# A small extra read of fifteen partitions behind the first load of a row softmax

## The chip, the core and the metric

The kernel runs on one core of a Trainium2 chip. The metric is the device time of one execution in microseconds (us), as a median over runs. The core has several engines with their own instruction streams: VectorE (DVE), ScalarE (ACT), GpSimd (POOL) and SyncE (SP). Data moves between the chip's memory and the core's on-chip buffers by 16 DMA engines; SyncE and ScalarE issue the transfers here, each on a queue of its own.

## The reference

```
B, H, S = 2, 8, 2112
bias   = rel_bias[:, clip(pos[:, None] - pos[None, :], -16, 16) + 16]     # H x S x S
logits = logits + bias[None]                                              # B x H x S x S, float32
out    = softmax(logits, axis=-1)
```

There are 2 x 8 x 2112 = 33,792 rows of 2112 numbers. Each row gets a bias that depends only on the head and on the clipped distance between the row's position and the column, and then a softmax over the row. All data is float32: 285 MB are read and 285 MB written.

## The kernel before

The 33,792 rows are divided among 128 partitions, 264 rows (`ROWS`) in sequence on each. A step takes R = 6 rows of every partition: one load of 128 x 12,672 numbers into one of four buffers `X[0]` to `X[3]` (`NBUF` = 4), so that there are 44 steps, 11 passes over the four buffers. In each partition the load is one contiguous piece of 50,688 B.

The work of a step, with its lines:

- SyncE issues the load (`load`, L78). In the first pass it issues four loads back to back (L106); after that it waits for the buffer's previous store (`take(nc.sync, st[b], 16)`) and issues the next load into it. `take`, L74, is every wait on a semaphore that is counted down again.
- VectorE waits for the load (`ld[b]`), then adds the bias to each of the six rows and takes its maximum in the same instruction (`add`, L175). The bias comes from a strip `F` that is copied once per pass from a table in PSUM (L169).
- ScalarE takes the exponential of each row, with the row's sum (`exps`, L184).
- VectorE takes reciprocals and scales the rows in two halves (`scale`, L192 and L196).
- ScalarE waits for the six scaled rows and issues the store (`store`, L82). The last step's store is issued in two halves of three rows.

Everything happens in the order in which it is written on each engine. Loads lie on SyncE's DMA queue (q1 in the profile) and stores on ScalarE's (q10); both run on the same 16 DMA engines. A DMA raises its semaphore by 16 in all, and a buffer counts as loaded or stored at the full 16. Ahead of the loops, VectorE builds the bias table from `rel_bias`, which ScalarE loads (L100).

Of the kernel before, what the change touches and what calls it, by code (L numbers as in the profile page):

```python
# [15 lines left out]
def kernel(  # L16
# [6 lines left out]
    nc = tc.nc  # L23
    P = 128
    B, H, S, S2 = logits.shape
# [3 lines left out]
    ROWS = B * H * S // P  # L29
    PB = S // ROWS  # L30
    assert ROWS * P == B * H * S and PB * ROWS == S and PB == H == 8
    R = 6
    NBUF = 4
# [4 lines left out]
    MW = S + ROWS - 1  # L38
    FW = S + STEP - 1
    BIG = 3.0e38  # L40

    io = ctx.enter_context(tc.tile_pool(name="io", bufs=1))
    X = [io.tile([P, R * S], FP32, tag=f"X{b}", name=f"X{b}") for b in range(NBUF)]
# [9 lines left out]
    def view(t, offset, dims):  # L53

        return bass.AP(tensor=t.tensor, offset=t.offset + offset, ap=[[list(t.ap[0])[0], P]] + dims)

    def rows(t, j, n):

        return bass.AP(tensor=t.tensor, offset=t.offset + j * S, ap=[[ROWS * S, P], [1, n * S]])

    with tc.tile_critical(no_gpsimd_drain=True):  # L61
# [6 lines left out]
        rb = nc.alloc_semaphore("rb")  # L68
        idx = nc.alloc_semaphore("idx")
        dve = nc.alloc_semaphore("dve")  # L70
        landed = tc.alloc_semaphore("landed")

        def take(eng, sem, n):
            eng.wait_ge(sem, n).then_inc(sem, -n)  # L74


        def load(j, b):
            nc.sync.dma_start(out=X[b][:, :], in_=rows(logits, j, R)).then_inc(ld[b], 16)  # L78
# [15 lines left out]
        def settle():  # L94
# [6 lines left out]
            out=bass.AP(tensor=F.tensor, offset=F.offset, ap=[[PB * list(F.ap[0])[0], P // PB], [1, H * W]]),  # L101
            in_=bass.AP(
                tensor=rel_bias.tensor, offset=rel_bias.offset, ap=[[0, P // PB], [1, H * W]]
            ),
        ).then_inc(rb, 16)
        for n in range(NBUF):  # L106
            load(n * R, n)

        nc.gpsimd.iota(ip[:, 0], pattern=[[0, PB]], base=0, channel_multiplier=1).then_inc(idx, 1)
        nc.gpsimd.iota(ip[:, 2], pattern=[[1, PB]], base=0, channel_multiplier=0).then_inc(idx, 1)  # L110
# [16 lines left out]
        for m, op in ((eq, ALU.is_equal), (gt, ALU.is_gt), (le, ALU.is_le), (lt, ALU.is_lt)):  # L127
# [4 lines left out]
            out=view(F, 0, [[W, H], [1, W]]), in0=view(F, 0, [[W, H], [1, W]]),  # L132
# [8 lines left out]
                           in_=view(F, RT, [[Q, 2], [PB, Q // PB], [0, PB]])))  # L141
# [9 lines left out]
            out=view(F, 0, [[W, PB], [1, W]]), in0=view(F, SC + 2 * PB, [[1, PB], [0, W]]),  # L151
# [7 lines left out]
            out=view(M, U, [[ROWS, PB], [1, W]]), in0=view(F, 0, [[W, PB], [1, W]]),  # L159
            in1=view(F, SC + 8 * PB, [[1, PB], [0, W]]), op=ALU.add))  # L160
        then(v.tensor_copy(out=view(M, U + W, [[ROWS, PB], [1, ROWS - W]]),  # L161
                           in_=view(F, SC + 7 * PB, [[1, PB], [0, ROWS - W]])))
# [8 lines left out]
        def add(b):  # L171
            take(v, ld[b], 16)
            for r in range(b * R, (b + 1) * R):
                x = X[b][:, (r - b * R) * S : (r - b * R + 1) * S]
                v.tensor_tensor_reduce(  # L175
                    out=x, in0=x, in1=F[:, STEP - 1 - r : STEP - 1 - r + S], scale=-1.0, scalar=BIG,
                    op0=ALU.add, op1=ALU.min, accum_out=nmax[:, r : r + 1],
# [76 lines left out]
```

## Time and profile before

| | |
|---|---|
| median of 3 runs | 1332.47 us (1328.36 to 1335.96) |
| the profiled execution | 1331.85 us, of which the span of the trace is 1330.0 us |
| VectorE busy | 977.7 us (74%) |
| ScalarE busy | 574.3 us (43%) |
| moved by DMA | 570.99 MB, mean 429 GB/s over the span |
| a load, issue to landing | 37.4 us (median) |
| a store, issue to landing | 60.2 us (median) |

The span runs from the first to the last instruction; the execution's own time is 1.85 us longer. In a row of the sums by window, the columns are the window, its length, busy time and instruction count of DVE, ACT and POOL, the clock granted to TensorE (unused here), and the busy share and rate of the DMA engines. In the page's groups the time behind the last bar is how long the engine sat idle ahead of these instructions, and what ended it. A row of the timeline gives start, duration, engine, line and operation; a "q" behind an engine's name is its sequencer, which issues DMAs.

### The profile page before, as it was taken

To read this page: it belongs to the slowest core of one execution; us is meant where nothing else is said; L and a number is where in the kernel's file an instruction comes from. 1 tells how busy PE (TensorE), PEld (TensorE's weight loads), DVE (VectorE), ACT (ScalarE), POOL (GpSimd) and SP (SyncE) were. 2 spreads that over 40 slices of the span, in tenths; PEclk is the share of its full clock that TensorE was granted. 3 is DMA by queue.
4 is the path that set the end of the run, shared out by engine and by line. 5 is a ranking of instruction groups with operands and counts; after the bars stand their busy time and mean duration, and the time that the engine had idled before them with its cause. 6 is when DMAs were issued, how large, how long until landed. Compare 5 with 4: busy or idle time off the path is not lost. (4 is left out here: it accounts for less than half of the span.)

```text
span 1330.0 us, 2473 instructions
## 1 busy us (share of the span) xinstructions
DVE 977.7 (74%) x917; ACT 574.3 (43%) x538; POOL 0.4 (0%) x6
## 2 busy tenths in 40 slices
DVE  7998767677877776687778767677877777677773
ACT  3474333444444343344444333444444443333442
POOL 0000000000000000000000000000000000000000
DMA  9999999999999999999999999999999999999997
GB/s 414 416 436 427 430 438 439 433 425 434 439 436 431 428 436 436 439 431 424 439 438 434 430 430 436 439 433 430 430 438 434 427 428 438 436 438 428 428 438 308
DMA packets 12850, 570.99 MB, mean 429 GB/s; under 512 B 1440, under 2 KB 1456, under 8 KB 1456
## 3 DMA queue, kind: packets, MB, share of 16 engines
q1 hardware_dynamic: 6336, 285.48, 49.8%
q10 hardware_dynamic: 6512, 285.49, 49.6%
q14 instruction: 2, 0.02, 0.0%
HBM read 285.49 MB, written 285.47 MB: 429 GB/s over the span
## 5 line engine op out<-in xcount | busy, mean ns | idle before, releaser
L175 DVE CUSTOM_DVE_ANT_0 X<-X,F 128x2112 f32<-128x2112 f32 x264 | 605.2, 2354 | 310.1 <-DVEq L74 310.1
L184 ACT ACTIVATE X<-X,nmax 128x2112 f32<-128x2112 f32 x264 | 541.7, 2052 | 559.0 <-ACTq L74 539.0
L196 DVE TENSOR_SCALAR X<-X,rec 128x2112 f32<-128x2112 f32 x264 | 332.5, 1316 | 13.2
L184 ACT ACT_TABLE_LOAD x10 | 12.8, 1283 | 170.8 <-ACTq L74 170.8
L184 ACT ACTIVATION_READ_ACCUMULATOR X<-X,nmax 128x1 f32 x264 | 49.2, 186 | 0.0
L169 DVE COPY F<-M 128x2135 f32 x11 | 26.1, 2374 | 0.5 <-DVEq L198 0.5
L175 DVE DVE_READ_ACCUMULATOR2_ANT nmax<- 128x1 f32 x264 | 21.6, 82 | 0.0
L192 DVE RECIPROCAL rec<-tot 128x3 f32<-128x3 f32 x88 | 14.9, 170 | 0.0
L131 DVE TENSOR_TENSOR F<-F 128x264 f32<-128x264 f32 x1 | 0.4, 433 | 7.0 <-DMA F<-in_rel_bias_dram 7.0
L161 DVE COPY M<-F 128x1848 f32<-128x1848 f32 x1 | 2.1, 2077 | 0.0
L97 DVE MEMSET F<- 128x264 f32 x1 | 0.3, 278 | 1.1 <-SPq L61 1.1
L135 DVE TENSOR_REDUCE F<-F 128x33 f32<-128x264 f32 x1 | 0.6, 608 | 0.0
L158 DVE TENSOR_TENSOR M<-F 128x264 f32<-128x264 f32 x1 | 0.4, 441 | 0.0
L150 DVE TENSOR_TENSOR F<-F,rbS 128x264 f32<-128x264 f32 x1 | 0.4, 426 | 0.0
L128 DVE TENSOR_SCALAR F<-F 128x8 f32<-128x8 f32 x4 | 0.4, 165 | 0.0
L163 DVE COPY M<-rbS 128x247 f32<-128x247 f32 x1 | 0.4, 407 | 0.0
L143 DVE STREAM_TRANSPOSE F<-F 128x64 f32<-128x64 f32 x1 | 0.2, 246 | 0.0
L138 DVE STREAM_TRANSPOSE F<-F 128x64 f32<-128x64 f32 x1 | 0.2, 245 | 0.0
L148 DVE TENSOR_SCALAR F<-F,rbS 128x8 f32<-128x8 f32 x1 | 0.2, 231 | 0.0
L154 DVE SCALAR_TENSOR_TENSOR F<-F,rbS 128x8 f32<-128x8 f32 x1 | 0.2, 227 | 0.0
L149 DVE TENSOR_SCALAR F<-F,rbS 128x8 f32<-128x8 f32 x1 | 0.2, 225 | 0.0
L155 DVE SCALAR_TENSOR_TENSOR F<-F,rbS 128x8 f32<-128x8 f32 x1 | 0.2, 221 | 0.0
(15 smaller groups left out, 2.1 us busy)
## 6 DMA issues: line engine op xcount, KB each, us to landing
X<-in_logits_dram SPq DMA_DIRECT2D x44, 6336.0 KB, 37.4
out_dram<-X ACTq DMA_DIRECT2D x43, 6336.0 KB, 60.2
out_dram<-X ACTq DMA_DIRECT2D x2, 3168.0 KB, 17.3
F<-in_rel_bias_dram ACTq DMA_DIRECT2D x1, 16.5 KB, 8.0
```

The lines of the kernel that those rows point to most:

```text
L128: then(v.tensor_scalar(out=m, in0=dp, scalar1=0.0, scalar2=None, op0=op))
L131: then(v.tensor_tensor(out=view(F, 0, [[W, H], [1, W]]), in0=view(F, 0, [[W, H], [1, W]]), in1=view(F, SC + 3 * PB, [[1, H], [0, W]]), op= ...
L135: then(v.tensor_reduce(out=F[:, RB : RB + W], in_=view(F, 0, [[1, W], [W, H]]), axis=mybir.AxisListType.X, op=ALU.add))
L150: then(v.tensor_tensor(out=view(F, 0, [[W, PB], [1, W]]), in0=view(F, SC + 2 * PB, [[1, PB], [0, W]]), in1=view(rbS, W - 1, [[0, PB], [-1, ...
L158: then(v.tensor_tensor(out=view(M, U, [[ROWS, PB], [1, W]]), in0=view(F, 0, [[W, PB], [1, W]]), in1=view(F, SC + 8 * PB, [[1, PB], [0, W]] ...
L161: then(v.tensor_copy(out=view(M, U + W, [[ROWS, PB], [1, ROWS - W]]), in_=view(F, SC + 7 * PB, [[1, PB], [0, ROWS - W]])))
L163: then(v.tensor_copy(out=M[:, 0:U], in_=low.to_broadcast([P, U])))
L169: v.tensor_copy(out=F[:, :], in_=M[:, bass.ds(ROWS - STEP - j, FW)]).then_inc(dve, 1)
L175: v.tensor_tensor_reduce(out=x, in0=x, in1=F[:, STEP - 1 - r : STEP - 1 - r + S], scale=-1.0, scalar=BIG, op0=ALU.add, op1=ALU.min, accum_ ...
L184: nc.scalar.activation(out=x, in_=x, func=EXP, scale=-1.0, bias=nmax[:, r : r + 1], accum_out=tot[:, r : r + 1],).then_inc(expd, 1)
L192: v.reciprocal(out=rec[:, r0 : r0 + HALF], in_=tot[:, r0 : r0 + HALF]).then_inc(inv, 1)
L196: v.tensor_scalar_mul(out=x, in0=x, scalar1=rec[:, r : r + 1]).then_inc(scaled, 1)
```

## The change

Behind load 0, SyncE issues one more DMA. It reads 2,560 numbers (10,240 B) for each of fifteen partitions, 32, 36, and so on to 88, into `X[3]`: the first part of what load 3 brings to these partitions. Load 3 comes after loads 1 and 2 as before, but now behind a wait for a new semaphore `even`, which the extra DMA raises. Load 3 overwrites the same places with the same data, so that the extra DMA adds nothing to the result.

```diff
+    LOW, PAD = 32, 2560
 ...
+        even = nc.alloc_semaphore("even")
 ...
-        for n in range(NBUF):
+        load(0, 0)
+        pad = X[NBUF - 1]
+        nc.sync.dma_start(
+            out=bass.AP(tensor=pad.tensor, offset=pad.offset + LOW * list(pad.ap[0])[0],
+                        ap=[[4 * list(pad.ap[0])[0], 15], [1, PAD]]),
+            in_=bass.AP(tensor=logits.tensor, offset=logits.offset + (LOW * ROWS + (NBUF - 1) * R) * S,
+                        ap=[[4 * ROWS * S, 15], [1, PAD]]),
+        ).then_inc(even, 16)
+        for n in range(1, NBUF - 1):
             load(n * R, n)
+        take(nc.sync, even, 16)
+        load((NBUF - 1) * R, NBUF - 1)
```

On SyncE, ahead of its loop, the instructions of before stand like this (`X_58` to `X_61` are the four buffers `X[0]` to `X[3]`; the branch behind them enters the loop):

```order
L249 UNCONDITIONAL_BRANCH
L78 DMA X_58<-in_logits_dram 128x12672
L78 DMA X_59<-in_logits_dram 128x12672
L78 DMA X_60<-in_logits_dram 128x12672
L78 DMA X_61<-in_logits_dram 128x12672
L97 UNCONDITIONAL_BRANCH
```

And after the change, with the line numbers of the changed kernel:

```order
L261 UNCONDITIONAL_BRANCH [waits SP_sequencer_49]
L80 DMA X_58<-in_logits_dram 128x12672
L110 DMA X_61<-in_logits_dram 15x2560
L80 DMA X_59<-in_logits_dram 128x12672
L80 DMA X_60<-in_logits_dram 128x12672
L80 DMA X_61<-in_logits_dram 128x12672 [waits even]
L99 UNCONDITIONAL_BRANCH
```

Loads 1 to 3 stand one place further back, and the load into `X_61` waits; the other engines' instructions, and SyncE's loop, are as before.

## The prediction

> **What bounds the kernel now.** I read the page first: the line of GB/s over the span, the DMA queues, and the groups of lines with what ended their idle time.
>
> ```profile
> span 1330.0 us, 2473 instructions
> ...
> DMA  9999999999999999999999999999999999999997
> ...
> q1 hardware_dynamic: 6336, 285.48, 49.8%
> q10 hardware_dynamic: 6512, 285.49, 49.6%
> ...
> L175 DVE CUSTOM_DVE_ANT_0 X<-X,F 128x2112 f32<-128x2112 f32 x264 | 605.2, 2354 | 310.1 <-DVEq L74 310.1
> ...
> X<-in_logits_dram SPq DMA_DIRECT2D x44, 6336.0 KB, 37.4
> out_dram<-X ACTq DMA_DIRECT2D x43, 6336.0 KB, 60.2
> ```
>
> The 16 DMA engines are busy from end to end, half of their time for loads (q1) and half for stores (q10). VectorE waits 310.1 us in front of its add (L175), released each time through L74, the wait for a load. So the transfers are the bound. The second view, the sums by window, gives their pace, and shows start and end.
>
> ```profile
> 0.00:42.00 42.00, 32.20 (x48) 13.63 (x13) 0.42 (x6) 1.00 0.96 406
> 300.00:500.00 200.00, 149.29 (x138) 88.57 (x84) 0.00 (x0) 1.00 1.00 434
> ...
> 1.95:2.30 0.35, 0.32 (x6) 0.00 (x0) 0.00 (x0) 1.00 7.14 2172
> 2.30:3.00 0.70, 0.16 (x3) 0.00 (x0) 0.00 (x0) 1.00 0.00 0
> 3.00:3.10 0.10, 0.00 (x0) 0.00 (x0) 0.00 (x0) 1.00 1.41 507
> ...
> 1322.20:1324.20 2.00, 0.00 (x0) 0.00 (x0) 0.00 (x0) 1.00 0.12 51
> 1324.40:1328.80 4.40, 0.00 (x0) 0.00 (x0) 0.00 (x0) 1.00 0.05 23
> 1328.80:1330.00 1.20, 0.00 (x0) 0.00 (x0) 0.00 (x0) 1.00 0.00 0
> ```
>
> The last two columns are the DMA engines' busy share and the GB/s, counted at the packets' starts. In the middle the engines move 434 GB/s at a share of 1.00. At the start, a packet is one partition's 6336.0 KB / 128 = 50,688 B. From 1.95 to 2.30 us, 2172 GB/s x 0.35 us = 760 KB: fifteen packets. Then nothing starts until 3.00, and 507 GB/s x 0.10 us is one packet. So one engine begins about 1 us after fifteen others. At the end a share of 0.12 is two engines of 16, and about 0.06 is one: fourteen engines are done by 1322.2 us, a fifteenth by 1324.4, and the sixteenth works alone until 1328.8. The bytes are the same for each engine, so the last one is about 6.6 us behind the fourteen, and the end waits for it.
>
> Where does it fall behind? A load counts as landed when its last engine is done, so the late engine sets when VectorE starts, and so when ScalarE issues the store. The timeline of ScalarE has these issues, one per buffer.
>
> ```profile
> 135.70 0.34 ACTq L82 DMA_DIRECT2D out_dram<-X  x1
> ...
> 316.30 0.34 ACTq L82 DMA_DIRECT2D out_dram<-X  x1
> ...
> 675.60 0.34 ACTq L82 DMA_DIRECT2D out_dram<-X  x1
> ...
> 1190.40 0.34 ACTq L82 DMA_DIRECT2D out_dram<-X  x1
> ...
> 1280.08 0.34 ACTq L82 DMA_DIRECT2D out_dram<-X  x1
> ```
>
> One load and one store at 434 GB/s take 2 x 6,488,064 B / 434 GB/s = 29.90 us; call it a step. From 135.70 to 316.30 are 6 steps: 180.60 us, 1.2 more than 6 x 29.90. The next 12 take 359.30, 0.5 more. The 17 to 1190.40 take 514.80, 6.5 more. The last 3 take 89.68, nothing more. In total 8.2 us over 38 steps. The pace of all engines together stays at 434, yet the pace of the latest one slips, and in bouts: that is the only sizeable loss after the start.
>
> **The change part by part.** *The extra DMA itself.* Fifteen rows of 10,240 B, behind load 0 and ahead of load 1 on SP's queue. One engine's share of 434 GB/s is 27.1 GB/s, so a row takes 0.38 us on its engine; none of the rows here is of that size. The nearest above is the first packet of an engine, from the start's window: 7.14 x 0.35 x 16 / 15 = 2.67 us for five times the bytes, 0.54 us at that rate. Below, no engine that carries a row can gain by it. I take 0.38, since the queue is already running when the rows come (bounds 0.38 to 0.54). Fifteen engines thereby do everything later by that, and one does not: the 1 us by which the late one started becomes 0.6.
>
> Which engines take the rows is not seen in this trace. By the Trainium skill (DMA: Bandwidth & Descriptors, "Why a DMA increments its semaphore by 16 and not by 1"), a DMA of SyncE runs on the largest number up to 16 that divides its slowest dimension, on the lowest-numbered engines: fifteen here, one each. No run here shows it yet. That the sixteenth is the one that starts late is my inference.
>
> *SP's queue.* One more issue ahead of loads 1 to 3, then the wait for `even` ahead of load 3.
>
> ```profile
> L78 SPq DMA_DIRECT2D X<-in_logits_dram x44: 332/333/737, 1.0 to 1250.7; - x44
> ...
> SPq L74 <- SPq L74: 131.6, 3, 72.8
> ...
> 40.65 2.35 DVE L175 CUSTOM_DVE_ANT_0 X<-X,F 128x2112 f32<-128x2112 f32 x1
> ...
> 84.06 2.35 DVE L175 CUSTOM_DVE_ANT_0 X<-X,F 128x2112 f32<-128x2112 f32 x1
> ...
> 113.67 2.36 DVE L175 CUSTOM_DVE_ANT_0 X<-X,F 128x2112 f32<-128x2112 f32 x1 [5.54 <-DVEq L74]
> ```
>
> An issue takes 0.33 us, and loads 1 and 2 are only queued behind load 0 then. The wait ends when the rows have landed: load 0 occupies about 2 us plus 6.49 MB / 434 GB/s = 15 us, so at about 19 us, issue included. Queued behind the wait on SP are load 3 and the loop's first wait for a store; that wait lasts 72.8 us anyway (the longest of SP's), so SP is free. Loads 1 and 2 are another 30 us of transfers, so the engines still have work until about 48 us when load 3 joins at 19. VectorE starts on load 1 at 40.65 and on load 3 at 84.06 without a wait; its first wait for data after load 0 is at 113.67. Cost of issue and wait: 0. If load 3 joined only after load 2 had drained, the cost would be the gap, up to a load's latency.
>
> *The lag.* The lag grew by 1.2 us in the first bout, little for 12 steps, then 6.5. My reading: being behind is what makes an engine slower, since its packets then meet the others' turn from one buffer or direction to the next. An engine that starts 0.6 us back instead of 1 sits inside the field, and the chain to the long bout does not start. Then no engine ends later than the fourteen did, give or take a packet. The sum on the profiled execution: last packet at 1322.2 + 0.38 for the rows + 1.2 from there to the span's end = 1323.8, against 1330.0: -6.2 us. Also the fourteen idled shortly before the end, because the last store came late:
>
> ```profile
> 1305.00:1307.50 2.50, 2.35 (x4) 0.00 (x0) 0.00 (x0) 1.00 0.57 243
> ```
>
> 0.43 of 2.5 us is 1.1 us of mean idle time, which goes too when the last load no longer lands late. Together -7.3 us. The steps say the same from the other side: 8.2 - 0.38 = 7.8 if all the slip goes, 7.0 if the 1.2 of the first bout stays. The profiled execution took 1331.85 us, 1.85 more than its span; it becomes 1324.55. It lies 0.6 below the median of 1332.47, so the forecast is 1325.2 us, -0.55%.
>
> **The rivals.** *The lag has another cause, and nothing changes (0.20).* The late engine may be slow by itself, or be slowed by which addresses it reads at that time, whatever its phase. Then it does the same packets with the same losses, its own queue is not longer, and the end stays: 1332.5 us. For it: the slip comes in bouts, as addresses go by. Against a steady handicap: twelve steps in a row cost only 0.5 us more than the engines' mean pace, which an always slower engine could not do.
> The Trainium skill (DMA: Bandwidth & Descriptors, "Latency and other measured facts") has engines 7 and 15 as usually slower than the rest, with a best guess at the cause that concerns the software queue alone. By that rule 15 stays last; the page shows only hardware queues and instruction fetches here, so its guessed cause is absent, and the twelve steps speak against it.
>
> *The rows miss their mark (0.07).* If the late engine is among the fifteen, or the fifteen rows all lie on one or a few engines, the late one is delayed too: 1332.5 + 0.4 = 1332.9 us, up to 15 x 0.38 = 5.7 more if one engine carries all, and the load behind waits for it: 1338.2.
>
> *Another phase is worse: slower (0.18).* What decides may be the phase between one engine and the fifteen, not its sign. The place is the long bout. Its mean price is 6.5 / 17 = 0.38 us a step, and in its steepest part
>
> ```profile
> 886.44 0.34 ACTq L82 DMA_DIRECT2D out_dram<-X  x1
> ...
> 1129.94 0.34 ACTq L82 DMA_DIRECT2D out_dram<-X  x1
> ```
>
> 8 steps take 243.50 us, 4.3 over 239.2, so 0.54 each. If the new phase meets this price from the start, 38 steps cost 14.4 to 20.5 us instead of 8.2: 1338.7 to 1344.8 us, about 1341. It decides for "slower" from (8.2 + 6.7) / 38 = 0.39 us a step. For it: the three runs of before already lie between 1328.36 and 1335.96, so the slip varies by some 4 us each way without a change.
>
> **How the numbers follow.** The forecast's case has 0.55. Its own range goes from 1324.3 (all 8.2 us gone) to 1328.1, where the late engine is cured but the fifteenth, done at 1324.4, stays: 1324.4 against 1328.8 is -4.4. Half a per cent, about what a measurement of this kernel can tell from no change, is 6.7 us, so the threshold is 1325.8, inside this case: 0.45 of its 0.55 fall below, 0.10 within. With the 0.20 and the 0.07 that is 0.37 for the same. Slower has 0.18. The range reaches from 1322.0 (1324.3, with half of the lower spread of before's runs) to 1341.0, the middle of the slower case.
>
> **What would show it.** In the profile after, right would be: one engine's packets alone in the last microseconds gone, so that the DMA share falls from near 1 to 0 within about 3 us of the end; store issues 29.9 to 30.0 us apart all the way; a DMA of 15 rows that lands near 19 us; no wait of VectorE ahead of its second to fourth buffer. Wrong would be: the same long tail at a share of 0.06 with the last packet near 1329, or steps of 30.3 us and more again, or from early on.

## The result, and the profile after

| | before | after |
|---|---|---|
| median | 1334.87 us (9 runs, 1328.36 to 1336.56) | 1327.46 us (9 runs, 1326.46 to 1328.63) |
| the profiled execution | 1331.85 us, span 1330.0 | 1327.58 us, span 1325.7 |

The ratio is 0.9946, with a 95% interval from 0.9932 to 0.9961: faster by 0.54%. The spreads matter as much as the medians. Three more sets of runs of the kernel before, made beside the experiments, hold 31, 35 and 35 runs from 1326.37 to 1338.20 us, and 17, 16 and 16 of them lie over 1332 us; the others lie mostly between 1326 and 1330. I call these the upper and the lower group. The change has no run over 1328.63. It does not make the best executions faster; it removes the upper group. The profiled execution of before lies between the two groups, so the two traces differ by 4.3 us of span where the medians differ by 7.4.

The sums by window of the changed kernel show the end:

```profile
1305.00:1307.50 2.50, 2.48 (x3) 0.00 (x0) 0.00 (x0) 1.00 1.06 456
1320.70:1322.40 1.70, 0.00 (x0) 0.00 (x0) 0.00 (x0) 1.00 0.17 75
1322.80:1324.40 1.60, 0.00 (x0) 0.00 (x0) 0.00 (x0) 1.00 0.07 32
1324.50:1325.70 1.20, 0.00 (x0) 0.00 (x0) 0.00 (x0) 1.00 0.00 0
```

No engine idles at 1305 us any more (share 1.06, counted at the packets' starts, where before had 0.57). At 1320.7 us some three engines of 16 are left (0.17), and one alone works from 1322.8 (0.07) until about 1324.4: a tail of nearly 4 us, where before the last engine had trailed by 6.6. The store issues in ScalarE's timeline show where the tail stopped growing:

```profile
137.96 0.34 ACTq L84 DMA_DIRECT2D out_dram<-X  x1
...
320.21 0.34 ACTq L84 DMA_DIRECT2D out_dram<-X  x1
...
679.73 0.34 ACTq L84 DMA_DIRECT2D out_dram<-X  x1
...
1188.10 0.34 ACTq L84 DMA_DIRECT2D out_dram<-X  x1
...
1277.67 0.34 ACTq L84 DMA_DIRECT2D out_dram<-X  x1
```

The first 6 steps take 182.25 us, 2.9 more than 6 x 29.90. The next 12 take 359.52, much as before. The 17 to 1188.10 take 508.37, just 17 x 29.90; before they took 514.80. The long bout is gone. The DMA issues on the two pages hold the clue to why. Before:

```profile
X<-in_logits_dram SPq DMA_DIRECT2D x44, 6336.0 KB, 37.4
out_dram<-X ACTq DMA_DIRECT2D x43, 6336.0 KB, 60.2
```

and after:

```profile
X<-in_logits_dram SPq DMA_DIRECT2D x44, 6336.0 KB, 40.9
out_dram<-X ACTq DMA_DIRECT2D x43, 6336.0 KB, 56.4
...
X<-in_logits_dram SPq DMA_DIRECT2D x1, 150.0 KB, 17.5
```

The last column is the median time from issue to landing. Loads land 3.5 us later and stores 3.8 us earlier, in the median over the run. An engine that alternates between the queues moves one packet of each in 2 x 1.87 us (50,688 B at 27.1 GB/s), so this is about an offset of one packet: the two streams stand differently against each other on at least one engine. One engine is enough for that, because a load has landed only when its last engine is done. Where it happened is seen in the DMA packets that start between 46.4 and 48.3 us, soon after the first store was issued. Before:

```profile
DMA packets 16, 0.81 MB, mean 427 GB/s; under 512 B 0, under 2 KB 0, under 8 KB 0
...
q10 hardware_dynamic: 16, 0.81, 98.5%
```

and after:

```profile
q10 hardware_dynamic: 15, 0.76, 92.4%
q1 hardware_dynamic: 1, 0.05, 9.0%
```

Before, all 16 engines start a store packet (q10) there. After, one engine is reading (q1) while the others store: between 44.95 and 46.4 us one store packet had already started, where before no packet starts at all:

```profile
q1 hardware_dynamic: 1, 0.05, 11.8%
q10 hardware_dynamic: 1, 0.05, 8.1%
```

The engines then alternate: from 48.3 to 50.2 us, 15 of them start a load packet and one a store packet, so the one keeps its offset. A load raises its semaphore in 16 steps, whose times are in the trace. For load 2, which lands next, 15 of them come by 53.80 us and the last at 55.94; before, all 16 had come by 53.62. I call this a split meeting.

### The profile page after: what moved, and what is told of

Read it like the earlier page. It is cut to its first block, busy times and chain, and to the rows that moved or that the text cites. A ratio compares the mean times of both kernels' runs of the same rounds, so it can differ in the third digit from the quotient of the medians.

```text
span 1325.7 us, 2475 instructions
## 1 busy us (share of the span) xinstructions
DVE 977.9 (74%) x917; ACT 574.3 (43%) x538; POOL 0.4 (0%) x6
## 6 DMA issues: line engine op xcount, KB each, us to landing
X<-in_logits_dram SPq DMA_DIRECT2D x44, 6336.0 KB, 40.9
out_dram<-X ACTq DMA_DIRECT2D x43, 6336.0 KB, 56.4
X<-in_logits_dram SPq DMA_DIRECT2D x1, 150.0 KB, 17.5
```

## The experiments

Three sets of runs on three chips follow; each ratio compares a variant with the runs of the kernel before in its own set. In the variants with extra rows the change's DMA is written as a function, `again(partition, step, rows, column, length)`; where only a number differs, the diff shows it as it would stand in the change.

Theories at first: *lateness* (the prediction's: the late sixteenth engine is given its start back), *issue or wait*, *any extra bytes*. After the first four, one more: the *meeting* theory, by which only the offset between the load and the store stream counts. All variants keep the kernel's own work. "Delay" edits are made in the kernel before unless said otherwise. The two numbers behind each are the median landing times of loads and stores on its page.

**The rows made tiny.**

```diff
-    LOW, PAD = 32, 2560
+    LOW, PAD = 32, 128
```

> The fifteen rows are 512 B instead of 10,240 B, so that the issue, the semaphore and load 3's wait stay and the shift of fifteen engines falls from 0.38 us to about 0.02. Lateness theory (the engine that starts last must be given back its start): no gain, ratio to before 0.998 to 1.002, about 1334 us. Issue theory (the later load 3 or the extra issue does it, not the bytes): the gain stays, ratio 0.993 to 0.996, about 1327 us.

Measured: 1332.11 us, ratio 0.9989 (0.9964 to 1.0013), 6 of 12 runs over 1332; landings 37.5 and 60.3. Issue, semaphore and wait alone give no clear gain.

**Sixteen rows: every engine shifted alike.**

```diff
-                        ap=[[4 * list(pad.ap[0])[0], 15], [1, PAD]]),
+                        ap=[[4 * list(pad.ap[0])[0], 16], [1, PAD]]),
 ...
-                        ap=[[4 * ROWS * S, 15], [1, PAD]]),
+                        ap=[[4 * ROWS * S, 16], [1, PAD]]),
```

> Sixteen rows of 10,240 B instead of fifteen, so that every engine is shifted by the same 0.38 us. Lateness theory: the last engine stays as far behind the others as before, ratio 0.998 to 1.003, about 1334 to 1335 us, with a tail of one engine of some 5 us or more. Theory that any short transfer at this place helps by breaking the rhythm: ratio 0.993 to 0.996, about 1327 us.

Measured: 1327.06 us, ratio 0.9958 (0.9938 to 0.9977), 1 of 12 over 1332; landings 39.8 and 57.4. The gain is there with no engine given anything back: the lateness theory has failed. Between 44.95 and 46.4 us its packets are

```profile
q10 hardware_dynamic: 10, 0.51, 80.7%
q1 hardware_dynamic: 5, 0.25, 48.7%
```

ten store packets and five reads: ten of the 16 engines take the store a packet earlier than the others.

**Twice the rows' length.**

```diff
-    LOW, PAD = 32, 2560
+    LOW, PAD = 32, 5120
```

> Fifteen rows of 20,480 B, a shift of 0.76 us instead of 0.38. Lateness theory: the engine without a row is then about level with the first of the others, nobody is later than before by more than 0.4 us, so the time is that of the change within 0.4 us: about 1327 to 1328 us, ratio 0.993 to 0.996. Theory that one particular phase between the one and the fifteen decides: another phase gives another time, back toward 1334 us (ratio over 0.998) or lower than the change (ratio under 0.993).

Measured: 1329.42 us, ratio 0.9971 (0.9953 to 0.9988), 1 of 12 over 1332; landings 41.0 and 56.4. About half the gain. In the same window all 16 engines start the store, one packet earlier than before: the streams are offset, without a split.

**The change, and two engines made late.**

```diff
+        again(LOW, 4, 2, 2560, 5120)
 ...
-        take(nc.sync, even, 16)
+        take(nc.sync, even, 32)
```

> The change, and behind its fifteen rows two rows of 20,480 B more, on two engines, which are thereby 0.76 us later than the rest. Lateness theory: the lag comes back on one of these two, the time returns to that of before, ratio 0.997 to 1.003, about 1332 to 1336 us. Theory that the sixteenth engine alone is special: two other engines may be late without harm, the gain stays, ratio 0.993 to 0.996, about 1327 us.

Measured: 1327.28 us, ratio 0.9948 (0.9929 to 0.9967), 0 of 8 over 1332; landings 39.9 and 57.2. Two engines 0.76 us later than the rest do no harm: the second blow to lateness.

**Rows as long as a packet.**

```diff
-    LOW, PAD = 32, 2560
+    LOW, PAD = 32, 12672
```

> Fifteen rows of 50,688 B, the size of one packet of a load, so that fifteen engines are shifted by one whole packet (1.87 us) and their packet boundaries stand against the first store as in the kernel before. Theory of the meeting (what counts is where in its run of read packets an engine is when the first store reaches it, since engines then alternate between reading and writing): all or nearly all engines meet the store alike, as before, no gain from it, and the rows cost 1.9 us: ratio 0.999 to 1.004, about 1335 us. Theory that extra bytes at this place help as such: ratio 0.993 to 0.998, about 1328 us.

Measured: 1329.16 us, ratio 0.9986 (0.9966 to 1.0006), 1 of 12 over 1332. The first store is met alike (16 store packets from 46.4 to 48.3 us), but the landings are 40.1 and 57.3: the load queue is one packet longer on these engines, which offsets the streams from then on. I had not thought of that; I read the time as the lower group's plus most of the rows' own 1.9 us.

**VectorE held up, no extra reads.**

```diff
         settle()
+        then(v.memset(F[:, 0:470], 0.0))        # then 1065, then 1660
+        settle()
 
         def strip(j):
```

> The kernel before without any extra read; VectorE fills 470 numbers of the strip's buffer ahead of its loop (about 0.45 us), so that the first store is issued that much later while the loads run as before. Meeting theory: the boundaries stand 0.45 us earlier against the store, the other way from the change's 0.38, so no certain gain: ratio 0.995 to 1.003. Theory that extra bytes or a shift of the loads are needed: ratio 0.998 to 1.002, about 1334 us.

> The same with 1,065 numbers, about 0.95 us. Meeting theory: the first store meets the engines half a packet later in their reads than in the kernel before, and at one of the three delays (0.45, 0.95, 1.45 us) the engines must split, some taking the store one packet earlier than others; there the ratio is 0.992 to 0.997, about 1326 to 1329 us. Theory that extra bytes are needed: ratio 0.998 to 1.002, about 1334 us, at all three.

> The same with 1,660 numbers, about 1.45 us, which is a packet of 1.87 us less the change's shift of 0.38 to 0.42: the boundaries stand against the store as in the change. Meeting theory: the gain of the change without its bytes, ratio 0.992 to 0.996, about 1326 to 1329 us. Theory that extra bytes are needed: ratio 0.998 to 1.002, about 1334 us.

The first store is issued at 40.99 us before and at 41.12, 41.76 and 42.34 in these three. The shortest delay thus barely moved it. Measured: 1334.54 us (ratio 1.0004, 0.9976 to 1.0032), 1330.46 (1.0007, 0.9983 to 1.0031) and 1327.34 (0.9982, 0.9962 to 1.0003); over 1332 are 7, 5 and 1 of 12, against 16 of 35 of the kernel before beside them. The first two have landings of 37.3 and 60.2, 37.2 and 60.1. The third has

```profile
X<-in_logits_dram SPq DMA_DIRECT2D x44, 6336.0 KB, 34.4
out_dram<-X ACTq DMA_DIRECT2D x43, 6336.0 KB, 63.1
```

offset the other way, and from 46.4 to 48.3 us

```profile
q10 hardware_dynamic: 13, 0.66, 80.1%
q1 hardware_dynamic: 3, 0.15, 24.0%
```

three engines reading once more. A fill on VectorE that moves the first store by 1.35 us thus comes to the change's median without an added byte. Its ratio's interval just reaches 1, so the count over 1332 says more here than the ratio.

**The change, with the store put back.** The same fill, of 800 numbers, in the changed kernel; its first store is issued at 41.66 us instead of 41.11.

> The change, and VectorE fills 800 numbers ahead of its loop, so that the first store comes about 0.5 us later and meets the engines' packet boundaries as in the kernel before, all of them alike; the sixteenth engine still has its 0.38 us back. Meeting theory (a split meeting gives the gain): the two groups of runs of the kernel before are back, near 1327 and near 1335 us, median 1329 to 1335, at least 3 of 12 runs over 1332. Lateness theory (the sixteenth engine's start gives it): the change's times, all runs within 1326 to 1330 us.

Measured: 1333.32 us, ratio 1.0012 (0.9986 to 1.0039), 6 of 12 over 1332, in two groups (1326.63 to 1330.99 and 1335.65 to 1336.77). The rows are read as in the change, with the same 150 KB, and the gain is gone. The page has

```profile
X<-in_logits_dram SPq DMA_DIRECT2D x44, 6336.0 KB, 37.3
out_dram<-X ACTq DMA_DIRECT2D x43, 6336.0 KB, 60.2
...
X<-in_logits_dram SPq DMA_DIRECT2D x1, 150.0 KB, 17.5
```

the landings of the kernel before, and from 46.4 to 48.3 us all 16 engines start a store packet again:

```profile
q10 hardware_dynamic: 16, 0.81, 98.5%
```

This profile is of a run of the lower group (1328.64 us), and so is that of the 0.95 us delay (1327.76). Landings as in step are thus seen in short executions too; they do not tell which group an execution falls in. Of all the runs this one tells the theories apart best, with a reservation: the change was not run again in this set, and its 0 of 9 is from another one.

**Sixteen rows as long as a packet.** The rows' count 16 and length 12,672.

> Sixteen rows of 50,688 B: every engine one packet later, none ahead, and the first store met as in the kernel before. Against the fifteen rows of this size only the sixteenth engine differs. Lateness theory: two groups of runs, 1.9 us above those of the kernel before, near 1329 and 1337 us, median 1331 to 1337, some runs over 1335. Meeting theory with equal meeting also gives two groups, then the fifteen rows' lack of runs over 1334 stays unexplained by it; a result like the fifteen rows (all under 1334) would speak for the bytes or the wait instead.

Measured: 1330.30 us, ratio 0.9987 (0.9969 to 1.0006), all between 1328.23 and 1333.70; landings 44.7 and 52.6. As with the fifteen, no run is over 1334, so once more nothing is seen to hang on the sixteenth engine. Four of 12 are over 1332; less the rows' 1.9 us, none is over 1331.8. I expected two groups; with the streams offset by two packets (7.3 us in the landings) it has one wide one. It was not the equal meeting that I meant to make either: besides the longer load queue, one engine took the store a packet early, as in the change (15 store packets from 46.4 to 48.3 us). And its profiled execution (1332.85 us) has a DMA share of only 0.28 from 1305.0 to 1307.5 us, so offset streams are not free of the loss.

**A longer delay.** Two fills of 1,210 numbers; the first store is issued at 43.32 us.

> The kernel before with VectorE held up by about 2.3 us ahead of its loop (two fills of 1,210 numbers), a whole packet and some more, so that the first store finds all engines one read packet further on, but again all alike. Meeting theory: two groups of runs as in the kernel before, at least 3 of 12 over 1332 us, median 1328 to 1336. Theory that a later first store helps as such (the delay of 1.45 us did): all runs 1326 to 1330 us.

Measured: 1328.96 us, ratio 0.9984 (0.9961 to 1.0006), 4 of 12 over 1332 in a spread from 1326.95 to 1335.92; landings 37.3 and 60.8, close to before. So a late store is no clear gain as such; four of twelve against one of twelve is a weak difference by itself, but it goes with the landings. Its profiled execution (1335.92 us) shows the tail, in the sums by window:

```profile
1305.00:1307.50 2.50, 2.35 (x5) 2.37 (x3) 0.00 (x0) 1.00 0.14 61
...
1328.00:1332.80 4.80, 0.00 (x0) 0.00 (x0) 0.00 (x0) 1.00 0.06 26
```

Most engines wait at 1305 us for the last store (share 0.14), and one works alone up to 1332.8.

**Two engines late, no fifteen rows.** The change's DMA with 2 rows of 5,120 numbers.

> No fifteen rows; only two rows of 20,480 B, so that two engines are 0.76 us later and the other fourteen meet the store as in the kernel before. Lateness theory: engines that are late from the start become the stragglers every time, the lower group vanishes: median 1333 to 1338 us, ratio 1.000 to 1.006. Meeting theory: as before, or better if the two split off: ratio 0.994 to 1.001.

Measured: 1329.82 us, ratio 1.0002 (0.9978 to 1.0026), 4 of 12 over 1332 (all four over 1336); landings 38.7 and 58.3. The lower group has not vanished, against lateness. The two late engines did split off in the profiled execution (2 store packets between 44.95 and 46.4 us), and yet the upper group is there: with two of sixteen the meeting is not enough, or does not come about in every run.

## Why the prediction was right, and where its reason was not

*The time.* 1325.2 us was forecast and 1327.46 measured, in the range; -0.55% and -0.54%. The agreement is partly luck: the sum on the profiled execution gave -7.3 us, and that pair of traces has -4.3. It misses 3.0 us because it let all engines end with the fourteen, while one still trails until 1324.4. The medians differ by 7.4 because the runs of before lie higher than its profiled one: the median of the nine is 1334.87, that of the three from which the forecast set out 1332.47. Of the signs that the prediction named, the rows' landing near 19 us came; the others did not all come. One engine still works alone at the end, the first six steps are 30.4 us apart, and VectorE waits ahead of its fourth buffer.

Two of its sums are slightly off by their own terms, without weight for the result: 7.0 for the steps with the first bout kept leaves out the 0.38 (6.6), and the lower bound of the range would be 1322.2, not 1322.0.

*What bounds the kernel, and where it loses.* Right. In the two traces the gain is the bout from 675 to 1190 us (6.5 us before, nothing after) and, with it, the idle time at 1305 us. The small growth in the first steps did not go: 1.2 us before, 2.9 after.

*The costs of the extra read.* Right in that they cost nothing in the end, but not in the detail. VectorE still starts its second buffer without a wait; for the fourth, which the prediction saw ready too, it waits 1.75 us:

```profile
40.77 2.35 DVE L187 CUSTOM_DVE_ANT_0 X<-X,F 128x2112 f32<-128x2112 f32 x1
...
86.01 2.36 DVE L187 CUSTOM_DVE_ANT_0 X<-X,F 128x2112 f32<-128x2112 f32 x1 [1.75 <-DVEq L76]
```

SyncE's wait for `even` is not the reason: with the tiny rows, which keep it, VectorE starts this buffer at 83.98 us without a wait. Of load 3's 16 semaphore steps, 15 come by 83.95 us and the last at 85.83, later than any of before's (83.58); that it is the engine of the split meeting is likely, but not shown. The DMA engines stay busy meanwhile (433 GB/s at a share of 1.00 from 60 to 120 us).

The rows landed 17.5 us after an issue at 1.4 us, at 18.9, as worked out. One size was off: this DMA's issue on SyncE took

```profile
L110 SPq DMA_DIRECT2D X<-in_logits_dram x1: 982/982/982, 1.4 to 1.4; - x1
```

0.98 us instead of 0.33; SyncE had nothing else to do. The packets that start from 17.4 to 18.8 us in the changed kernel are

```profile
DMA packets 62, 0.96 MB, mean 689 GB/s; under 512 B 31, under 2 KB 31, under 8 KB 31
```

31 of them small. A load has 16 small packets beside its 128 rows (6,336 packets for 44 loads are 144 each), so 16 belong to load 0 and 15 to the rows. So the rows ran on fifteen engines, as the Trainium skill (DMA: Bandwidth & Descriptors, "Why a DMA increments its semaphore by 16 and not by 1") has it. Which fifteen, no run shows.

*The step that failed* is the one under "The lag": that an engine 0.6 us back instead of 1 sits inside the field and so escapes. Sixteen rows, which leave every engine as far back as it was, had the gain. The change with its store delayed by 0.55 us kept the fifteen rows and lost it. And a delay of VectorE by 1.45 us had no run but one over 1332 with no rows at all. The traces show it directly in the times at which the 16 semaphore steps of a store come. In the store that lands at 676 us, the last step is 2.2 us behind the median of the 16 before the change and 2.1 us after it, so the last engine had not moved into the field. In the one that lands at about 1280 us it is 12.3 us behind before and 3.4 us after. What went is the later growth, not the lateness. What the rows do, by the runs, is to move the engines' packet boundaries against the first store, by an estimated 0.38 us. The prediction noted that packets of the late engine meet "the others' turn from one buffer or direction to the next"; the turn counted, the early lateness did not.

*The rivals.* "Another phase is worse" had the right quantity, the phase, and the wrong sign and object: not one engine against fifteen, but loads against stores. The rule on engines 7 and 15 in the Trainium skill (DMA: Bandwidth & Descriptors, "Latency and other measured facts") does not by itself explain the upper group of runs: it goes with the change and comes back with 0.55 us on ScalarE's first store, and no engine was spared any work by that delay. Whether the engine that ends last is one of these two, no run shows.

*What stays open.* Six kernels have landings near 37.3 and 60.2 (before, tiny rows, 0.45, 0.95 and 2.3 us of delay, the change with its store put back), and all six have many runs over 1332: 28 of 60 in the five variants, 49 of 101 for before. Of the eight with other landings, six have at most 1 run there; the two others are the sixteen whole packets, which pay 1.9 us, and the two late engines. That the time of the first store against the loads decides, and not a head start of one engine, is shown by the store put back and by the 1.45 us delay, as far as 12 runs each can show it. That the landings sort the kernels is seen only afterwards, and the two late engines fit it badly. Why streams in step let one engine fall ever further behind in about half of the executions, and offset ones less often, is not shown; nor how many engines must be offset, since each kernel has one profile. No variant beat the change beyond the intervals.

## What to carry to other kernels

When two DMA streams share the engines and fill them, compare the spread of the runs before the medians, and look at the median landing times of both streams: a small edit that moves the first meeting of the streams can decide which group of runs a kernel is in. Such a gain is fragile: here a fill that moved the first store by 0.55 us took it away, and one that moved it by 1.35 us gave it to the kernel before, while shifts by 0.13, 0.77 and 2.33 us gave no clear gain. Test a reason by a variant that keeps the edit and removes its supposed effect; here two such runs, the sixteen rows and the store put back, overturned a theory whose number had come out right.

## What the runs showed of the hardware beyond expectation

How the two queues met at about 45 us still shows in the median landing of 44 loads: 34.4 us with three engines one read further, 37.3 in step, 40.9 with one engine's store a packet early, 44.7 with that and a longer load queue. The steps are 3 to 4 us, while the sum of both landings stays at 97.3 to 97.6 in these four.

And the same kernel varies by 0.9% (1326.43 to 1338.20 us in one set of 31 runs), with the engines' rate in mid-run the same in a short and a long execution (433 to 434 GB/s from 300 to 500 us). How far one engine falls behind goes with it. Six profiles are of kernels with the streams in step. In the four executions of 1331.85 to 1335.92 us, the last semaphore step of the store that lands at about 1280 us is 12.3 to 21.4 us behind the median step; in the two of 1327.76 and 1328.64 us it is 4.1 and 4.8 us behind. In the longest of them the loss shows twice: most engines idle at 1305 us ahead of the last store (the share of 0.14 above), and one engine then ends last.
